# A matmul kernel's first input load issued as two transfers, of partitions 0 to 15 and 16 to 127

## The chip, the core and the metric

The kernel runs on one core of one Trainium2 chip. The metric is the device time of one execution in microseconds (us). Beside the timed runs there is one execution that the hardware profiler recorded; all rows and windows are from it, with times counted from the start of its span.

## The reference

```python
batch, m, k, n = 16, 512, 1024, 768      # all inputs float32, scale = 0.1
return (scale * np.matmul(x, weight) + add_value).astype(np.float32)
```

The 16 x 512 rows of `x` are one matrix of 8192 rows. It is multiplied by a 1024 x 768 weight, scaled, and added to an addend of 8192 x 768. Read are 33.6 MB of `x`, 3.1 MB of weights and 25.2 MB of addends; 25.2 MB are written.

## The kernel before

**Tiles.** A tile is 128 rows of `x`, one on each partition; there are 64. Partition p holds 16 rows that follow each other in memory, so a load of 8 tiles reads 8 x 4 KB = 32 KB in one run for each partition. `xs` holds 16 tiles of `x` (line 68), in four quarters of four tiles; `ao` holds 32 tiles of addends, which become results in place (line 70).

**Stages.** ScalarE (ACT) and GpSimd (POOL) are the *movers*: `mover` (lines 148 to 162) loops over turns of 16 tiles, and in a turn over the four quarters `q`. For each quarter it waits for `x_sem[q]` (line 153, the load) and `turned` (line 154, free space in `va`), and then issues eight casts that bring a quarter of `x` to bf16 in another order (line 161). VectorE (DVE) casts the weights (`cast_w`, line 167), then transposes the moved data in 32 x 32 blocks (`turn`, line 171) and later combines product and addend (`finish`, line 181). TensorE (PE) multiplies: eight weight loads and 16 matmuls for a tile (`product`, line 205; the loop at line 221). VectorE's first `turn` needs the first quarter of both movers, and TensorE needs all the weights and the first `turn`.

**Order of the transfers.** Nearly all transfers are issued by SyncE (SP), in the order of `STREAM` (line 22): `w` weights, `a` addends, `x` tiles, `o` stores, each with its first tile and count. `sync_engine` (line 95) waits ahead of a transfer for what must be free or ready, and adds 16 to a semaphore when the transfer has landed. For a load of eight tiles, `x_sem` of its first quarter counts the landing, and the semaphore of its second quarter is raised at once when it is issued (lines 145 and 146). GpSimd stores the two tiles 8 and 15 by itself, in three bands of 6, 98 and 24 partitions (`BY_POOL`, line 31).

**The first load.** Tiles 0 to 7 (`FIRST`) are not in `STREAM`. Their load is issued by SP ahead of the joined section (`tc.tile_critical`, line 240), at line 237; at line 240 SP then joins the other engines. It covers 128 partitions with 32 KB each, and raises `x_sem[0]` when it has landed. `x_sem[1]`, the semaphore of the second quarter, is raised for this load by TensorE at line 217. The last store, of tiles 60 to 63, is issued behind the section at line 252.

Of the kernel before, what the change touches and what calls it, by code (L numbers as in the profile page):

```python
# [8 lines left out]
P = 128  # L9
# [7 lines left out]
VA_BUFS = 2  # L17
MOVE = 4
AHEAD = 4
HALF_BLOCK, PAST, SYNC_AT = 64, 4, 4  # L20

STREAM = [
# [12 lines left out]
def kernel(  # L35
# [8 lines left out]
    nc = tc.nc  # L44
# [12 lines left out]
    x_v = x_f.rearrange("(g p t) k -> p g t k", p=P, t=R)  # L57
# [4 lines left out]
    def rows(view, s, n):  # L62
        assert s // R == (s + n - 1) // R
        return view[:, s // R, s % R:s % R + n, :]
# [12 lines left out]
    x_sem = [tc.alloc_semaphore(f"x{i}") for i in range(X_SLOTS // MOVE)]  # L77
# [70 lines left out]
    def mover(eng, copy, parity, count, go=None, first=0, turns=T // X_SLOTS):  # L148
        if go is None:
            eng.preload_act_table(mybir.ActivationFunctionType.Copy)  # L150
        with eng.Fori(16 * (first + 1), 16 * (first + turns) + 1, 16) as i:  # L151
            for q in range(X_SLOTS // MOVE):
                eng.wait_ge(x_sem[q], i)
                eng.wait_ge(turned, i + (4 * q - 12) if q < 3 else i)  # L154
                if go is not None:
                    eng.sem_inc(go, 1)
                k = MOVE * q
                src = xs[:, k:k + MOVE, :].rearrange("p i (c b k) -> p (i c) b k", b=4, k=64)
                for a in (parity, parity + 2):
                    for b in range(4):  # L160
                        copy(va[q % VA_BUFS][32 * b:32 * b + 32, :, a, :],  # L161
                             src[32 * a:32 * a + 32, :, b, :]).then_inc(count, 1)
# [42 lines left out]
    def product(eng, acc, x_j, w_j, j):  # L205
        eng.ldweights(x_j, tile_position=(0, 0))  # L206
        for n0, n1 in ((0, CUT), (CUT, N)):
            m = eng.add_instruction(mybir.InstMatmult(  # L208
                start_tensor_calc=(j == 0), stop_tensor_calc=(j == KJ - 1),
                tile_size=(P, P), tile_position=(0, 0), ldweights=False,  # L210
                name=nc.get_next_instruction_name(), engine=eng.engine,
                ins=[eng.lower_ap(w_j[:, n0:n1]), eng.lower_ap(x_j, for_matmul_weights=True)],
                outs=[eng.lower_ap(acc[:, n0:n1])]))
        return m

    def tensor_engine(eng):
        eng.sem_inc(x_sem[1], 16)
        eng.sem_inc(turned, TURNED)
        eng.sem_inc(made, MADE)
        eng.wait_ge(casts, KJ)  # L220
        with eng.Fori(TURNED + 2, TURNED + 2 + T, XT_TILES) as i:
            for q in range(XT_TILES):
                if q % 2 == 0:
                    eng.wait_ge(turned, i + q if q else i)
                    eng.wait_ge(made, i + q if q else i)
                for j in range(KJ):
                    x2 = xt[:, q, j // 2, :].bitcast(bf16).rearrange("p (m r) -> p r m", r=2)
                    m = product(eng, mm[:, q, :], x2[:, j % 2, :], w_bf[:, j, :], j)
                if q % 2:
                    m.then_inc(done, 4)  # L230
# [3 lines left out]
        eng.addr_align(HALF_BLOCK, offset=PAST, max_nops=0)  # L234
    s, n = FIRST
    place = dataclasses.replace(xs[:, s:s + n, :], dep_tracking_offset=P * X_SLOTS * K)
    first = nc.sync.dma_start(place, rows(x_v, s, n))
    first.then_inc(x_sem[0], 16)
    tc.no_tile_sem_insts.add(first.ins.name)
    with tc.tile_critical(no_gpsimd_drain=True):  # L240
        sync_engine(nc.sync)
        mover(nc.scalar, nc.scalar.copy, 0, by_act)
        mover(nc.gpsimd, nc.gpsimd.tensor_copy, 1, by_pool, pool_go, 0, TURN_AT)
        nc.gpsimd.wait_ge(made, MADE + PAIR.stop)
        for p, n in BY_POOL:
            store_pair(nc.gpsimd, p, n)
        nc.gpsimd.addr_align(HALF_BLOCK, offset=PAST, max_nops=0)
        mover(nc.gpsimd, nc.gpsimd.tensor_copy, 1, by_pool, pool_go, TURN_AT, T // X_SLOTS - TURN_AT)
        vector_engine(nc.vector)
        tensor_engine(nc.tensor)  # L250
    s, n = LAST
# [36 lines left out]
```

## Time and profile before

| what | value |
|---|---|
| median of 3 runs | 208.18 us (208.10 to 208.29) |
| the profiled execution's own time | 208.1 us |
| its span | 206.3 us |
| mean granted TensorE clock | 0.981 |
| bytes moved over the span | 87.04 MB, 422 GB/s |

The span is what the profiler saw between the first and the last instruction; the execution's own time holds 1.8 us more, around it. Busy shares are over the span. A row of a timeline has the start, the duration, the engine (SPq is SP's queue of issues), the line in the program, the operation, the output and the input, and in brackets the idle time before it with what ended it. A row of the chain has the start, the duration and what the time was spent on. An issue row is the time that SP takes to issue; the data move later.

### The profile page before, as it was taken

The page shows a single profiled execution, that of the slowest core. Times are in us where ns is not written, and L with a number is a line of the kernel's source. Part 1 is how long each engine was busy: PE and PEld are TensorE (multiplying, and loading weights), DVE is VectorE, ACT ScalarE, POOL GpSimd, SP SyncE. Part 2 cuts the span into 40 slices and gives each one's busy share as a digit, 9 for nine tenths or more (in the row PEclk, how much of TensorE's full clock was granted, in tenths as well). Part 3 has the DMA queues.
Part 4 walks back from the last instruction along what each step waited for, and adds up shares of the span by engine and source line. Part 5 has one row for each costly group of instructions (what it writes and reads, how often), then busy time and mean ns, then how long its engine had stood idle before and what let it go on. Part 6 is the DMA issues. An engine that isn't in the chain of part 4 may idle for free.

```text
span 206.3 us, 2222 instructions
## 1 busy us (share of the span) xinstructions
PE 168.5 (82%) x1008; PEld 50.5 (24%) x512; DVE 98.0 (48%) x66; ACT 134.7 (65%) x129; POOL 137.4 (67%) x135
## 2 busy tenths in 40 slices
PE   0000099999999999999999999999999999999800
PEld 0000023322333333223333322233333222333200
DVE  0005523555555555555555555555554655455320
ACT  2049970799999807999999069999990199910000
POOL 0049994699999906999999459999991199920000
PEclk9999999999999999999999999999999999999975
DMA  7989999999999999999999999999999999999986
GB/s 299 413 378 467 400 483 407 419 438 464 407 457 457 407 407 407 407 457 408 437 434 423 447 424 434 432 419 443 438 415 429 429 437 443 429 457 419 457 367 281
DMA packets 4065, 87.04 MB, mean 422 GB/s; under 512 B 480, under 2 KB 480, under 8 KB 1120
## 3 DMA queue, kind: packets, MB, share of 16 engines
q1 hardware_dynamic: 3856, 86.25, 97.7%
q0 software_dynamic: 208, 0.79, 0.9%
q14 instruction: 1, 0.01, 0.0%
HBM read 61.87 MB, written 25.17 MB: 422 GB/s over the span
## 4 chain that ended last, share of the span: by engine, by line
DMA 37%; PE 37%; POOL 10%; ACT 5%; issue 4%; DVE 2%; SPq 1%; POOLq 0%; DVEq 0%; ACTq 0%
PE mm L208 37%; DMA out_dram<-ao 22%; DMA xs<-in_x_dram 15%; POOL va L161 9%; ACT va L161 5%; DVE xt L176 1%; DVE ao L185 1%; POOL out_dram L93 1%; SPq L128 0%; SPq L116 0%; DVEq L174 0%; SPq L100 0%; POOLq L154 0%; POOLq L151 0%; DVEq L185 0%
## 5 line engine op out<-in xcount | busy, mean ns | idle before, releaser
L208 PE MATMUL mm<-w_bf,xt 128*128 128x256 bf16 (+1 forms) x1008 | 168.5, 328 | 27.1 <-DVE xt L176 26.2
L161 POOL CAST va<-xs 32x1024 bf16<-32x1024 f32 x128 | 135.2, 1056 | 44.3 <-DMA xs<-in_x_dram 30.6
L161 ACT CAST va<-xs 32x1024 bf16<-32x1024 f32 x128 | 133.4, 1042 | 45.3 <-DMA xs<-in_x_dram 41.7
L185 DVE SCALAR_TENSOR_TENSOR ao<-mm,ao 128x1536 f32 (+1 forms) x32 | 56.2, 1757 | 76.7 <-PE mm L208 73.6
L206 PEld LDWEIGHTS <-xt 128*128 128x128 bf16 x512 | 50.5, 99 | 144.5 <-issue 117.6
L176 DVE STREAM_TRANSPOSE xt<-va 128x1024 f32<-128x1024 f32 x32 | 39.4, 1234 | 4.6 <-POOL va L161 2.4
L169 DVE CAST w_bf<-ao 128x3072 bf16<-128x3072 f32 x2 | 4.6, 2276 | 18.0 <-DMA ao<-in_weight_dram 18.0
L150 ACT ACT_TABLE_LOAD x1 | 1.3, 1283 | 1.3 <-SPq L240 1.3
L93 POOL DMA_DIRECT2D out_dram<-ao x3 | 2.0, 672 | 0.0
L269 POOL MEMSET const-float32-0.0<- 128x1 f32 x1 | 0.1, 97 | 0.2 <-issue 0.2
L269 POOL MEMSET const-bfloat16-1.0<- 128x1 bf16 x1 | 0.1, 100 | 0.0
L269 POOL MEMSET const-float32-1.0<- 128x1 f32 x1 | 0.1, 98 | 0.0
L269 POOL MEMSET const-uint8-127<- 128x1 uint8 x1 | 0.1, 98 | 0.0
## 6 DMA issues: line engine op xcount, KB each, us to landing
xs<-in_x_dram SPq DMA_DIRECT2D x7, 4096.0 KB, 20.9
ao<-in_add_value_dram SPq DMA_DIRECT2D x6, 3072.0 KB, 16.0
out_dram<-ao SPq DMA_DIRECT2D x3, 3072.0 KB, 27.4
ao<-in_add_value_dram SPq DMA_DIRECT2D x1, 6144.0 KB, 24.2
out_dram<-ao SPq DMA_DIRECT2D x1, 6144.0 KB, 31.2
out_dram<-ao SPq DMA_DIRECT2D x1, 4608.0 KB, 14.7
xs<-in_x_dram SPq DMA_DIRECT2D x2, 2048.0 KB, 21.1
ao<-in_weight_dram SPq DMA_DIRECT2D x2, 1536.0 KB, 16.8
```

Of the source, the lines that this page charges most:

```text
L93: eng.dma_start(out_v[p:p + n, 0, PAIR, :], ao[p:p + n, PAIR, :]).then_inc(aside_sem, 16)
L150: eng.preload_act_table(mybir.ActivationFunctionType.Copy)
L161: copy(va[q % VA_BUFS][32 * b:32 * b + 32, :, a, :], src[32 * a:32 * a + 32, :, b, :]).then_inc(count, 1)
L169: eng.tensor_copy(w_bf[:, s:s + n, :], ao[:, W_AT + s:W_AT + s + n, :]).then_inc(casts, n)
L176: eng.transpose(xt[:, 2 * half:2 * half + 2, :, :].rearrange("p i c m -> p (i c m)"), va[move % VA_BUFS][:, q:q + 2 * KC, :, :].bitcast(fp ...
L185: eng.scalar_tensor_tensor(a, mm[:, q:q + 2, 0:N], float(scale), a, op0=mybir.AluOpType.mult, op1=mybir.AluOpType.add).then_inc(made, 2)
L206: eng.ldweights(x_j, tile_position=(0, 0))
L208: m = eng.add_instruction(mybir.InstMatmult(start_tensor_calc=(j == 0), stop_tensor_calc=(j == KJ - 1), tile_size=(P, P), tile_position=(0 ...
L269: nc = _bacc.Bacc("TRN2", target_bir_lowering=False, num_devices=1)
```

## The change

The load of tiles 0 to 7 is issued as two transfers, both by SP and both ahead of the joined section: partitions 0 to 15 (512 KB) with `x_sem[0]`, and partitions 16 to 127 (3584 KB) with `x_sem[1]`. The movers wait for `x_sem[0]` and `x_sem[1]` ahead of the first quarter and for no load ahead of the second. TensorE no longer raises `x_sem[1]`.

```diff
+HEAD = 16
...
         with eng.Fori(16 * (first + 1), 16 * (first + turns) + 1, 16) as i:
             for q in range(X_SLOTS // MOVE):
-                eng.wait_ge(x_sem[q], i)
+                for j in ((0, 1), (), (2,), (3,))[q]:
+                    eng.wait_ge(x_sem[j], i)
                 eng.wait_ge(turned, i + (4 * q - 12) if q < 3 else i)
...
     def tensor_engine(eng):
-        eng.sem_inc(x_sem[1], 16)
         eng.sem_inc(turned, TURNED)
...
     s, n = FIRST
     place = dataclasses.replace(xs[:, s:s + n, :], dep_tracking_offset=P * X_SLOTS * K)
-    first = nc.sync.dma_start(place, rows(x_v, s, n))
-    first.then_inc(x_sem[0], 16)
-    tc.no_tile_sem_insts.add(first.ins.name)
+    for i, part in enumerate((slice(0, HEAD), slice(HEAD, P))):
+        first = nc.sync.dma_start(place[part], rows(x_v, s, n)[part])
+        first.then_inc(x_sem[i], 16)
+        tc.no_tile_sem_insts.add(first.ins.name)
```

## Prediction, made before the result was known

> **What bounds the kernel now.** I read the page from the top: busy shares, the slices, the DMA queues. Then come windows over the start, the middle and the end, the chain, and the issues on SP in order of time.
>
> ```profile
> PE 168.5 (82%) x1008; PEld 50.5 (24%) x512; DVE 98.0 (48%) x66; ACT 134.7 (65%) x129; POOL 137.4 (67%) x135
> ...
> PEclk9999999999999999999999999999999999999975
> DMA  7989999999999999999999999999999999999986
> ...
> q1 hardware_dynamic: 3856, 86.25, 97.7%
> q0 software_dynamic: 208, 0.79, 0.9%
> ```
>
> The transfers take 98.6% of what 16 queues can carry in the span, and only the first and the last slices are below 9. No engine comes near that over the span. The windows say the same stage by stage (columns: window, its length, busy time of each engine, granted clock, DMA share, GB/s; a packet is counted where it starts, so a share can pass 1.00).
>
> ```profile
> 1.00:13.00 12.00, 0.00 (x0) 0.00 (x0) 0.00 (x0) 1.36 (x2) 0.00 (x0) 1.00 0.93 382
> 13.00:26.00 13.00, 0.00 (x0) 0.00 (x0) 5.83 (x4) 12.71 (x13) 12.39 (x10) 1.00 1.03 437
> 26.00:195.50 169.50, 168.45 (x1008) 50.54 (x512) 90.46 (x62) 120.66 (x116) 124.77 (x122) 1.00 1.00 430
> 195.50:201.00 5.50, 0.02 (x1) 0.00 (x0) 1.76 (x1) 0.00 (x0) 0.00 (x0) 0.78 0.98 424
> 201.00:203.00 2.00, 0.00 (x0) 0.00 (x0) 0.00 (x0) 0.00 (x0) 0.00 (x0) 0.50 0.99 424
> 203.00:205.00 2.00, 0.00 (x0) 0.00 (x0) 0.00 (x0) 0.00 (x0) 0.00 (x0) 0.50 0.75 320
> ```
>
> Two things run without a gap. The DMA share is 1.00 from 26 to 195.5 us and 0.98 or more up to 203. And TensorE is busy for 168.45 of the 169.50 us between its first and its last matmul, at clock 1.00. Both start behind the first load:
>
> ```profile
> 0.74 12.08 DMA xs<-in_x_dram
> ...
> 26.03 10.86 PE mm L208 x50
> ...
> 195.63 1.76 DVE ao L185
> ```
>
> These are rows of the chain: the load of tiles 0 to 7 lands at 12.82, the movers then start, TensorE starts at 26.03. The end is DMA's:
>
> ```profile
> 0.74 0.38 SPq L237 DMA_DIRECT2D xs<-in_x_dram  x1
> 1.39 0.90 SPq L109 DMA_DIRECT2D ao<-in_weight_dram  x2
> 2.34 0.58 SPq L128 DMA_DIRECT2D ao<-in_add_value_dram  x1
> 2.96 0.45 SPq L116 DMA_DIRECT2D xs<-in_x_dram  x1
> ...
> 197.67 0.33 SPq L252 DMA_DIRECT2D out_dram<-ao  x1
> ```
>
> When the last store, 1.57 MB, is issued at 197.67, the windows still have 5.33 us at 424 GB/s up to 203 and 2 us at 320 behind it, 2.26 + 0.64 = 2.9 MB. So 1.3 MB of earlier stores stand ahead of it, some 3.1 us: TensorE has that much slack at the end. **What the reader is to see:** a queue that never runs dry passes any delay at its head to the end one for one; time won at the head is passed on too. TensorE's start moves with the same load, so it does not become a new limit. The whole change lies in how soon, and how fast, the first 4 MB go in.
>
> **The change part by part.** The profiled execution took 208.1 us with a span of 206.3; the 1.8 us around it are kept. The median of the three runs is 208.18, 0.08 above. All sums are made against 208.1.
>
> 1. *Waits.* A turn of a mover had four waits on x semaphores, one for each quarter, and has four again: two at the first quarter, none at the second, one at each of the others. On SP, a full eight-tile load already raises the second quarter's semaphore at issue, so the added wait at the first quarter asks for nothing that is late in turns two to four. Behind it on ACT and GpSimd stand only the same quarter's casts. A wait on the chain costs hundredths:
>
> ```profile
> 12.84 0.04 ACTq L154
> ```
>
> In the worst case two waits in a row cost 0.04 us more for each of four turns; the queues are ahead by far more than that, so I take 0. TensorE loses one semaphore increment ahead of a wait that lasts until 26.03: 0.
>
> 2. *One more issue on SP.* The order of instructions is the same on all engines but SP, which gets a transfer of 16 x 8192 and one of 112 x 8192 for the one of 128 x 8192. The present issue takes 0.38 us, so weights, addends and tiles 8 to 15 are issued about 0.4 us later. What hides it: their data queue behind the first load, which lands only at 12.82, and SP is done issuing at 3.41. Without that cover it would be 0.4 us. The joined section is also entered 0.4 us later, and ACT's table load with it:
>
> ```profile
> 1.34 1.28 ACT L150 ACT_TABLE_LOAD   x1 [1.34 <-SPq L240]
> 12.92 17.05 ACT L161 CAST va<-xs 32x1024 bf16<-32x1024 f32 x16 [10.30 <-DMA xs<-in_x_dram]
> ```
>
> It would end at 3.0 instead of 2.62, 10 us ahead of its use: 0.
>
> 3. *The start of the queues.* Fine windows show how they start now:
>
> ```profile
> 0.00:1.70 1.70, 0.00 (x0) 0.00 (x0) 0.00 (x0) 0.36 (x1) 0.20 (x4) 1.00 0.00 0
> 1.70:1.80 0.10, 0.00 (x0) 0.00 (x0) 0.00 (x0) 0.10 (x1) 0.00 (x0) 1.00 4.58 1311
> 1.80:2.00 0.20, 0.00 (x0) 0.00 (x0) 0.00 (x0) 0.20 (x1) 0.00 (x0) 1.00 2.83 819
> 2.00:2.20 0.20, 0.00 (x0) 0.00 (x0) 0.00 (x0) 0.20 (x1) 0.00 (x0) 1.00 2.21 655
> 2.20:2.40 0.20, 0.00 (x0) 0.00 (x0) 0.00 (x0) 0.20 (x1) 0.00 (x0) 1.00 0.96 328
> 2.40:2.70 0.30, 0.00 (x0) 0.00 (x0) 0.00 (x0) 0.22 (x1) 0.00 (x0) 1.00 0.25 109
> 2.70:3.50 0.80, 0.00 (x0) 0.00 (x0) 0.00 (x0) 0.00 (x0) 0.00 (x0) 1.00 0.00 0
> ```
>
> 1311 GB/s x 0.1 us is 131 KB, four packets of 32 KB (one partition's eight tiles). The next windows hold five, four, two and one: 16 first packets, one for each queue, start between 1.7 and 2.7, with a mean of about 2.0. If 16 short lists reach all queues as soon as the first is reached now, the mean start comes 0.25 us and the last 0.8 us sooner; at the least nothing is gained. The queues rejoin at the end, so the worth lies between these: 0 to 0.8, and 0.4 if half of the spread goes.
>
> 4. *Where the first transfer goes.* This is the term that decides, and no row shows it: every load and store on SP's queue covers all 128 partitions. The first transfer uses 16 queues on 16 neighbouring partitions. The case's rows bound it from both sides. The 4.19 MB of the whole load take 9.75 us at 430 GB/s; the 0.52 MB of the first transfer take 1.22 at the same pace, the second's 3.67 MB take 8.53. **Lower end, 0:** a queue's pace is its own, wherever it writes. **Upper end:** a partition takes in no more than its 1/128 of the rate that all together show. Then 16 partitions take 53.8 GB/s and 9.75 us, 8.53 more; and the second, on 112 of 128, takes 9.75 instead of 8.53, 1.22 more; together +9.75. For the lower end speaks that the store of two tiles that GpSimd issues in bands of 6, 98 and 24 partitions shows no slower queue: 0.79 MB in 0.9% of 16 x 206.3 us is 27 GB/s for one queue, as the 86.25 MB in 97.7% give for the others. But most of it is the band of 98, it reads SBUF instead of writing it, and it runs between packets of other transfers. For the upper end speaks that the total never stays above the 430 GB/s that all 16 queues and all 128 partitions give together: nothing shows that a sixteenth of the queues could push more than a sixteenth of the total into one place, and here two queues and more would have to go into each eight partitions. Neither end has a row near it, so I take the middle, **+4.9 us**, with part 3's gain within its error (the queues' first packets would be held up anyway).
>
> [...]
>
> Sum: 208.1 + 4.9 = **213.0 us**. A queue that is held by its first packet cannot pass it, so the second transfer and the weights wait behind; the first tiles land at about 17.7 and TensorE starts at about 30.9.
>
> **The rivals.**
>
> *The queues start sooner and nothing holds them (the other side: faster).* It decides if the first transfer's 16 packets take their 1.2 us each. Then part 3 is all: 208.1 - 0.4 = 207.7, with 207.3 as its bound. For it: DMA is the bound from its first packet on, so each tenth of a microsecond counts. Against it: the gain is a part of the 1.0 us between the first and the last start, and part 4 must cost nothing. [...]
>
> *Nothing that can be measured.* The queues start as they do now, since what takes the time is the way from the issue at 0.74 to the first packet after 1.7, whatever its length; or the 16 partitions are dealt to a few queues and the other queues begin with the second transfer at once, every queue with the bytes that it has now. 208.0, with 207.8 to 208.3.
>
> *A hole between the two transfers.* The second's issue would end near 1.5 instead of 1.12, so its packets are due from about 2.1 to 3.1. The windows show no second packet before 3.5 now. The hole opens only if the second issue takes over 0.4 us more than I reckon; it would cost about 0.5: 208.6.
>
> **How the numbers follow.** Held queues (213.0): 0.58. Sooner start by over 0.2%: 0.20. Nothing measurable: 0.17. A hole: 0.05. The likeliest is the first, with its own range 210.8 to 215.0 (+2.7 to +6.9; the ends near 0 and near +9.75 are each unlikelier than the middle, and beyond 215.0 I leave 0.07). The range for 8 in 10 reaches down over the rival without effect and most of the faster one, to 207.6, and leaves 0.07 above and about 0.06 below: **207.6 to 215.0**. About 0.2%, 0.4 us, is what a measurement of this kernel can tell from no change. Faster 0.20, same 0.17, slower 0.58 + 0.05 = 0.63.
>
> **What would show it.** Right: in fine windows from 1.7 us on, 16 packets start, and then almost none up to 4 to 7 us; the chain's first piece ends near 17.7 instead of 12.82, TensorE starts near 30.9 and stays without gaps, and the last store is issued near 202.6. The windows of the middle keep share 1.00 and 430 GB/s. Wrong: the second group of 16 packets starts at 3.5 or sooner and the first load lands at 12.8 or sooner; then the first rival holds if the first 16 starts lie closer together than 1.0 us, and the second if not. If the first load lands late but the end does not move, the idea of the full queue is what failed. If the movers' first casts of a turn wait longer for a load than they do now, with the load landed, part 1 is wrong.

## The result, and the profile after

| | before | after |
|---|---|---|
| median of the timed runs | 208.11 us (208.07 to 208.29) | 217.75 us (217.53 to 218.39) |
| ratio | | 1.046, 95% interval 1.0446 to 1.0474 |
| span of the profiled execution | 206.3 us | 215.8 us |

The changed kernel is 9.6 us slower. The direction was forecast, the size was not: 213.0 was said, with 207.6 to 215.0 as the range.

The page of the changed kernel, first the rows that answer to those of before:

```profile
PE 167.3 (78%) x1008; PEld 50.3 (23%) x512; DVE 98.1 (45%) x66; ACT 134.7 (62%) x129; POOL 137.4 (64%) x135
...
DMA  7999999999999999999999999999999999999985
GB/s 115 194 285 216 402 438 474 401 422 446 462 416 428 419 425 468 401 452 433 408 416 473 431 386 437 446 427 415 433 433 431 431 434 428 492 437 405 437 387 246
...
q1 hardware_dynamic: 3872, 86.25, 97.6%
```

The busy row of the DMA queues does not show what happened: it is 9 from the second slice on, as before, and 97.6% stands where 97.7% stood. The GB/s row shows it. The first four slices, 21.6 us, move 115 to 285 GB/s; from the fifth on it is the usual 400 and more. The queues are as busy as ever, and move about half as much. Windows over the same stretches of both kernels, first before, then after (columns as in the prediction's windows):

```profile
2.70:5.00 2.30, 0.00 (x0) 0.00 (x0) 0.00 (x0) 0.00 (x0) 0.00 (x0) 1.00 0.77 328
5.00:7.00 2.00, 0.00 (x0) 0.00 (x0) 0.00 (x0) 0.00 (x0) 0.00 (x0) 1.00 0.95 410
7.00:12.00 5.00, 0.00 (x0) 0.00 (x0) 0.00 (x0) 0.00 (x0) 0.00 (x0) 1.00 0.97 419
12.00:22.00 10.00, 0.00 (x0) 0.00 (x0) 3.96 (x2) 8.88 (x9) 8.57 (x7) 1.00 1.03 433
```

```profile
2.70:5.00 2.30, 0.00 (x0) 0.00 (x0) 0.00 (x0) 0.39 (x1) 0.00 (x0) 1.00 0.00 0
5.00:7.00 2.00, 0.00 (x0) 0.00 (x0) 0.00 (x0) 0.00 (x0) 0.00 (x0) 1.00 1.47 262
7.00:12.00 5.00, 0.00 (x0) 0.00 (x0) 0.00 (x0) 0.00 (x0) 0.00 (x0) 1.00 0.82 210
12.00:22.00 10.00, 0.00 (x0) 0.00 (x0) 0.00 (x0) 0.00 (x0) 0.00 (x0) 1.00 0.94 239
22.00:36.00 14.00, 0.00 (x0) 0.00 (x0) 5.84 (x4) 12.75 (x13) 12.35 (x10) 1.00 1.02 427
36.00:205.00 169.00, 167.29 (x1008) 50.32 (x512) 90.52 (x63) 120.69 (x116) 124.82 (x122) 1.00 1.01 433
```

A packet is counted where it starts. After the 16 first packets no second one starts between 2.7 and 5.0; before, they start in this stretch at 328 GB/s. That is the small first transfer. Then come 17 us at 210 to 262 GB/s with queues that are busy nearly all the time: that is the second transfer, and it loses more than the first, as the runs below price it. From 22 us on all is as before. The chain of the changed kernel shows how it is passed on:

```profile
1.18 21.61 DMA xs<-in_x_dram
36.07 9.71 PE mm L210 x50
...
205.14 1.76 DVE ao L187
```

The first load lands at 22.79 instead of 12.82 (9.97 later), TensorE starts at 36.07 instead of 26.03 (10.04 later), its last result is 9.51 later, and the span is 9.5 longer. Half a microsecond is won back behind TensorE's start (its first 50 matmuls take 9.71 us instead of 10.86); why, no run shows. No more is won back, since neither the queues nor TensorE have a gap.

### The profile page after: what moved, and what is told of

Read it like the earlier page. It is cut to its first block, busy times and chain, and to the rows that moved or that the text cites. A ratio compares the mean times of both kernels' runs of the same rounds, so it can differ in the third digit from the quotient of the medians.

```text
span 215.8 us, 2230 instructions
## 1 busy us (share of the span) xinstructions
PE 167.3 (78%) x1008; PEld 50.3 (23%) x512; DVE 98.1 (45%) x66; ACT 134.7 (62%) x129; POOL 137.4 (64%) x135
## 3 DMA queue, kind: packets, MB, share of 16 engines
q1 hardware_dynamic: 3872, 86.25, 97.6%
## 4 chain that ended last, share of the span: by engine, by line
DMA 40%; PE 34%; POOL 9%; ACT 5%; issue 3%; DVE 3%; SPq 1%; POOLq 0%; DVEq 0%; ACTq 0%
PE mm L210 34%; DMA out_dram<-ao 21%; DMA xs<-in_x_dram 19%; POOL va L163 9%; ACT va L163 5%; DVE xt L178 2%; DVE ao L187 1%; POOL out_dram L94 1%; SPq L129 0%; SPq L239 0%; SPq L117 0%; DVEq L176 0%; SPq L101 0%; POOLq L156 0%; POOLq L158 0%
## 6 DMA issues: line engine op xcount, KB each, us to landing
xs<-in_x_dram SPq DMA_DIRECT2D x1, 3584.0 KB, 21.6
```

## The experiments

Theory 1 was the prediction's: where in SBUF the 16 queues write at a time decides their pace. Against it stood that any second transfer or wait at the head costs, that any transfer of fewer than 128 partitions is slow, that the small first transfer alone is slow, and that the memory which is read decides. The ratios below are to the kernel before, run beside each.

### The waits alone

One load of 128 partitions, with the changed waits of the movers.

```diff
-    for i, part in enumerate((slice(0, HEAD), slice(HEAD, P))):
...
+    first = nc.sync.dma_start(place, rows(x_v, s, n))
+    first.then_inc(x_sem[0], 16)
...
+        eng.sem_inc(x_sem[1], 16)
```

> The changed kernel's waits of the movers alone (both semaphores at the first quarter, none at the second); one load of 128 partitions, and TensorE raises the second semaphore as before. All theories of the transfers: 208.1, within 0.1. If the waits cost anything: up to 0.3 more.

Measured: 208.13 us, ratio 0.9996 (0.9987 to 1.0005). The waits cost nothing; all of the loss is in the transfers.

### The same cut in bytes, by tiles

```diff
-HEAD = 16
+HEAD = 1
...
-    for i, part in enumerate((slice(0, HEAD), slice(HEAD, P))):
-        first = nc.sync.dma_start(place[part], rows(x_v, s, n)[part])
+    for i, part in enumerate((slice(0, HEAD), slice(HEAD, n))):
+        first = nc.sync.dma_start(place[:, part, :], rows(x_v, s, n)[:, part, :])
```

> The changed kernel, with the same two transfers of 512 KB and 3584 KB, the same issues, semaphores and waits, but cut by tiles: tile 0 on all 128 partitions, then tiles 1 to 7 on all 128. Theory 1 (the place in SBUF): nothing is lost, 207.8 to 208.5. Rival (a second transfer at the head, or the second wait, costs by itself): near 217.5.

Measured: 208.79 us, ratio 1.0029 (1.0017 to 1.0041), a little above what was expected. Two transfers of the same sizes cost 0.6 us, not 9.6, as long as each covers all partitions.

### The cut at 64, and the cut into even and odd partitions

```diff
-HEAD = 16
+HEAD = 64
```

> The changed kernel with the cut at partition 64 instead of 16. Theory 1: partitions 0 to 63 hold half of the ways in, so each half goes at half the pace and the first load lands near 22 us: 217 to 218. If what costs is the small first transfer of 16 partitions, the loss is less than with 16: 210 to 213.

Measured: 218.54 us, ratio 1.0497 (1.0481 to 1.0513), a little above what was expected; the first load lands at 23.58 us. The other cut into 64 and 64:

```diff
-    for i, part in enumerate((slice(0, HEAD), slice(HEAD, P))):
+    for i, part in enumerate((slice(0, P, 2), slice(1, P, 2))):
```

> The changed kernel with the load cut into the even and the odd partitions, 64 each: as many transfers, partitions and bytes as with the cut at 64, but each half lies on all of SBUF. Theory 1 (neighbouring partitions share a way in): the loss goes, 208.5 to 209, as with the cut by tiles. Rival (a transfer of fewer than 128 partitions is slow by itself): 218 to 219 as with the cut at 64.

Measured: 208.51 us, ratio 1.0022 (1.0011 to 1.0032). These two kernels have the same number of transfers, partitions, pieces and bytes, and the same waits. They differ in which partitions go together (and with them which rows of `x`), and that is worth 10 us. A small first transfer is not needed for the loss: with 64 and 64 it is even larger.

### The shapes one at a time

Twelve loads ahead of the kernel's first load, each waited for; the one below stands for all:

```diff
+        nc.sync.dma_start(xs[0:16, s:s + n, :], rows(x_v, s, n)[0:16]).then_inc(probe_sem, 16)
+        nc.sync.wait_ge(probe_sem, 32)
```

> The kernel before, with twelve loads of tiles 0 to 7 issued one at a time ahead of its own first load (each waited for; all are written over by the full load at the end), so that the time of each shape stands alone. Order: partitions 0-127; 0-15; 16-127; every 8th partition (16 of them); 0-15 from every 8th row block; every 8th partition from row blocks 0-15; 0-31; 0-63; every 2nd partition (64); 0-95; 0-111; 32-95. Theory 1, neighbouring partitions share a way into SBUF that carries about one queue's pace, so the place decides: 11 us for the 128; about 6 for 0-15 wherever its rows come from; clearly less, 3 to 4, for every 8th partition wherever its rows come from; 15 to 18 for 16-127; about 6 for 0-31 and 11 for 0-63; less than 11 for every 2nd partition. Theory 2, a transfer that is not 128 partitions is slow by itself: about 6 for every 8th partition as for 0-15, and the same for all the 64s. Theory 3, the memory that is read decides: 0-15 from every 8th row block is as fast as every 8th partition, and every 8th partition from row blocks 0-15 as slow as 0-15.

The kernel was executed once, in 328.81 us. In its chain each load is a row (start, duration), in the order above; the rows of 0.02 us of issue between them are left out here:

```profile
0.95 12.02 DMA xs<-in_x_dram
12.99 6.71 DMA xs<-in_x_dram
19.72 16.86 DMA xs<-in_x_dram
36.60 4.96 DMA xs<-in_x_dram
41.58 6.62 DMA xs<-in_x_dram
48.21 4.71 DMA xs<-in_x_dram
52.94 7.03 DMA xs<-in_x_dram
59.98 12.54 DMA xs<-in_x_dram
72.55 7.58 DMA xs<-in_x_dram
80.15 16.41 DMA xs<-in_x_dram
96.57 16.65 DMA xs<-in_x_dram
113.24 7.56 DMA xs<-in_x_dram
```

The first three rows are partitions 0 to 127, 0 to 15 and 16 to 127: a load of 112 partitions takes 4.84 us longer than one of all 128. The next three rows are 16 partitions each: every eighth, 0 to 15 filled from every eighth row block, and every eighth filled from row blocks 0 to 15. Where the rows come from hardly matters (6.71 and 6.62; 4.96 and 4.71); where they go does, though every eighth was expected to take 3 to 4 us and took 4.96. Partitions 0 to 63 and 32 to 95 are 64 each: the same size, 12.54 and 7.56. For a rate I take off 2.27 us, what a full load needs beyond its 9.75 us at 430 GB/s:

| partitions loaded | MB | issue to landing, us | GB/s without the 2.27 us |
|---|---|---|---|
| 0-127 | 4.19 | 12.02 | 430 |
| 0-15 | 0.52 | 6.71 | 118 |
| every 8th (16) | 0.52 | 4.96 | 195 |
| 0-31 | 1.05 | 7.03 | 220 |
| 0-63 | 2.10 | 12.54 | 204 |
| even ones (64) | 2.10 | 7.58 | 395 |
| 32-95 | 2.10 | 7.56 | 396 |
| 0-95 | 3.15 | 16.41 | 222 |
| 0-111 | 3.67 | 16.65 | 255 |
| 16-127 | 3.67 | 16.86 | 252 |

The rivals fall: the number of partitions does not decide (64 of them run at 204, 395 or 396 GB/s), and neither does the source for 16 partitions, the only size for which it was varied. 0 to 63 is no faster than 0 to 31 (204 and 220). And 0 to 111, which holds all of 32 to 95 and 48 partitions more, runs at 255 where 32 to 95 run at 396: that a shape is fast does not make a larger one around it fast. The way into SBUF that theory 1 speaks of, and what one carries, was the author's guess: these runs time whole shapes.

That the slow shapes simply use fewer queues is not the reason either, as the packets of the two kernels show. The 16 that start between 1.70 and 2.70, first before, then after:

```profile
1.70:2.70 1.00, 0.00 (x0) 0.00 (x0) 0.00 (x0) 0.92 (x1) 0.00 (x0) 1.00 1.73 524
```

```profile
1.70:2.70 1.00, 0.00 (x0) 0.00 (x0) 0.00 (x0) 0.89 (x1) 0.00 (x0) 1.00 3.64 524
```

A share of 3.64 of 16 queues over 1.00 us is 3.64 us of a queue for each of 16 packets; before it is 1.73. For the second transfer, 210 GB/s between 7 and 12 us are 32 packets of 32 KB in 0.82 of 16 x 5.00 us, 2.05 us of a queue for each; before, 419 GB/s are 64 packets in 0.97 of it, 1.21 for each. The queues are busy (97.3% from 5.0 to 22.8 us after), and each packet takes longer.

### The two transfers of the change, priced apart in the kernel

The kernel before, with one more transfer ahead of its first load:

```diff
+    extra = nc.sync.dma_start(
+        dataclasses.replace(xs[0:16, 8:16, :], dep_tracking_offset=2 * P * X_SLOTS * K), rows(x_v, 8, 8)[0:16])
+    extra.then_inc(extra_sem, 16)
...
+                need(extra_sem, 16)
                 move = eng.dma_start(xs[:, k:k + n, :], rows(x_v, s, n))
```

> The kernel before, with its first load in one piece, and one more transfer ahead of it: partitions 0 to 15 of tiles 8 to 15, which the next load of x writes again later (its issue waits for this one). It prices the small transfer of the change alone. Theory 1: its 0.52 MB hold the queues for 4.4 us, as it took 6.71 by itself where 2.3 of the 12.02 of a full load are not data: 212.4 to 213. Rival (a small transfer costs its bytes, and the loss is in the second one): 209.4.

Measured: 212.45 us, ratio 1.0201 (1.0184 to 1.0218), 4.28 above the 208.17 beside it. The bytes cost 1.22 at the full pace; 3.1 are lost. With `16:P` in place of `0:16`:

> The same with partitions 16 to 127 of tiles 8 to 15, which prices the second transfer of the change alone. Theory 1 with what the single loads showed: 16.86 less 2.3, +14.5, 222 to 223, which is 6 more than its bytes cost. Rival (only the first, small transfer is slow, and what follows it waits): its bytes at the full pace, +8.5, 216.7.

Measured: 222.19 us, ratio 1.0672 (1.0654 to 1.069), 14.02 more. The bytes cost 8.53; 5.5 are lost. So the small transfer loses 3.1 and the large one 5.5, together 8.6 of the 9.6. The single loads gave 3.2 and 6.1. About 1 us is missing. Part of it is what each run wins back behind the landing of the first load: by the landings, 17.48 and 27.19 against 12.82, the two lose 3.4 and 5.8, 9.3 of the 9.97. No run takes the rest apart.

### More shapes, stores, and sizes of pieces

> The kernel before with fourteen single transfers ahead of its first load, each waited for. Loads: partitions 0-127; 0-15; 64-79; 56-71; every 4th (32); 16-79; 64-127; the odd ones (64); 16-111; 8-127. Then stores of 3 KB pieces of what was loaded (the output is written again later): 0-127; 0-15; 16-127; the even ones. [...] If a store's reading of SBUF is held in the same way, 0-15 and 16-127 of the stores are slower than their bytes say, as with the loads (9.6, 4 to 5, 12 to 13, 6); if only writing is held, about 9.6, 3.2, 9, 6.

Measured, loads from issue to landing: 12.01, 6.90, 6.93, 6.67, 5.01, 12.60, 12.73, 7.48, 16.45 and 22.11 us. The loads of 64 to 79 and of 56 to 71 are as slow as 0 to 15 (6.93 and 6.67 beside 6.90), and every fourth, 32 partitions, takes 5.01 where 0 to 31 took 7.03. 16 to 79 and 64 to 127 (12.60 and 12.73) are like 0 to 63 of the first dozen (12.54), the odd ones (7.48) like the even ones (7.58), and 16 to 111 (16.45) like 0 to 95 (16.41). One stands out: 8 to 127, 120 partitions, takes 22.11, nearly twice as long as all 128; why, no run shows. That load and the four stores, of 0 to 127, 0 to 15, 16 to 127 and the even ones, in the chain (rows of issue left out):

```profile
87.89 22.11 DMA xs<-in_x_dram
110.03 9.31 DMA out_dram<-xs
119.36 5.16 DMA out_dram<-xs
124.53 9.97 DMA out_dram<-xs
134.52 5.83 DMA out_dram<-xs
```

Stores are held as well: an eighth of the bytes takes 5.16 us from partitions 0 to 15, half of them from the even ones 5.83. For stores no run varied where the rows go in memory. But 16 to 127 lose far less than as a load. To tell whether it was the size of the pieces or the direction:

> The kernel before with nine single transfers ahead of its first load, each waited for: a load of partitions 0-127 in pieces of 32 KB; loads in pieces of 3 KB of 0-127, 0-15, 16-127 (three quarters of the bytes); stores in pieces of 24 KB of 0-127, 0-15, 16-127, the even ones; the load of 16-127 in pieces of 32 KB again. It is to tell why stores of 16-127 lost less (9.97 beside 9.31) than loads (16.86 beside 12.02): piece size or direction. If long pieces let the queues collide: the loads of 3 KB pieces lose little with 16-127 (about 10 beside 9.6) and the stores of 24 KB much (13 to 14 beside 9.3). If writing SBUF is what collides: the 3 KB loads lose much (13 beside 9.6), the 24 KB stores little (10). 0-15 is held to about a quarter of the pace in all cases (4.5 to 5.5).

```profile
13.04 10.38 DMA xs<-in_x_dram
23.44 5.59 DMA xs<-in_x_dram
29.05 12.88 DMA xs<-in_x_dram
41.95 8.71 DMA out_dram<-xs
50.67 5.11 DMA out_dram<-xs
55.80 9.82 DMA out_dram<-xs
65.64 5.37 DMA out_dram<-xs
71.02 17.23 DMA xs<-in_x_dram
```

These are the loads of 0 to 127, 0 to 15 and 16 to 127 in pieces of 3 KB, then the stores of the same and of the even ones in pieces of 24 KB, then the load of 16 to 127 in pieces of 32 KB again (rows of issue left out). Short pieces do not save the load of 112 (12.88 beside 10.38), and long ones do not hurt the store more (9.82 beside 8.71). The direction decides: a load of 112 partitions loses much, a store of the same little. That it is the writing of SBUF, and not the reading of memory, fits the loads of 16 partitions, where the source hardly mattered, but was not shown for 112. The repeated load took 17.23 us beside 16.86, so a single load is known to some 0.4 us. The kernels of these two sections were executed once each, in 348.17 and 295.79 us.

### What the end hangs on

Tiles 0 to 3 and 4 to 7 as two transfers of all partitions, each quarter's casts waiting for its own:

```diff
-    for i, part in enumerate((slice(0, HEAD), slice(HEAD, P))):
-        first = nc.sync.dma_start(place[part], rows(x_v, s, n)[part])
+    for i, part in enumerate((slice(0, MOVE), slice(MOVE, n))):
+        first = nc.sync.dma_start(place[:, part, :], rows(x_v, s, n)[:, part, :])
...
-                for j in ((0, 1), (), (2,), (3,))[q]:
-                    eng.wait_ge(x_sem[j], i)
+                eng.wait_ge(x_sem[q], i)
```

> The kernel before with its first load cut into tiles 0 to 3 and tiles 4 to 7, each on all 128 partitions, and each quarter's casts waiting for their own part alone. It tells whether the end hangs on the queues or on TensorE's start. The first casts should start near 8 us instead of 12.9 and TensorE 0.5 to 2 us sooner (the weights hold it then). If the queues set the end, as the prediction read it: 208.2 to 208.8, the price of a cut and no gain. If TensorE's start sets it: 206.5 to 207.7.

Measured: 208.05 us, ratio 0.9993 (0.9984 to 1.0002). Its timeline:

```profile
8.06 17.04 ACT L161 CAST va<-xs 32x1024 bf16<-32x1024 f32 x16 [4.96 <-DMA xs<-in_x_dram]
...
23.45 6.79 PE L208 MATMUL mm<-w_bf,xt 128*128 128x512 bf16 x27 [23.45 <-DVE xt L176]
```

The casts start 4.9 us sooner and TensorE 2.6 us sooner (0.5 to 2 were expected), and the time does not move; nor is the last store issued sooner (198.04 instead of 197.67). An earlier start of TensorE is lost again: between 26 and 195 us it is busy for 166.01 of 169.00 us, with a DMA share of 1.01, where before it was busy for 168.45 of the 169.50 from 26 to 195.5. That it waits for transfers there, so that the queues set the pace, is a reading; no row here names the waits. No run delays TensorE alone, so the slack that the prediction read for it at the end is not tested. This cut cost nothing that can be measured, not even the price that was expected, unlike that of tile 0 alone (0.6 us) and the even and odd one (0.3). In the even and odd one the first load lands at 13.14 us instead of 12.82, about as much later as it loses: its first half takes SP 0.55 us to issue instead of 0.38, and 15 packets start between 1.7 and 2.7 us (492 GB/s) where before 16 did (524). Why tile 0 alone loses, no run shows. No run points to a version that beats the kernel before.

## Why the prediction was right or wrong

- *What bounds the kernel: right.* The queues never run dry, a delay at their head arrives at the end but for half a microsecond (9.97 late at the landing, 9.5 at the end), and an earlier start of TensorE alone is worth nothing (2.6 us sooner, ratio 0.9993). No run won time at the head of the queues, so that such a gain is passed on too was not shown. The 3.1 us of slack come from a mean rate that holds 2 us from before the last store's issue; from 197.67 on the trace has 8.63 us at 319 GB/s, 2.75 MB, which leaves 1.2 MB or 2.8 us. No run tests it.
- *Part 1, waits at 0: right*, by the kernel with the waits alone.
- *Part 2, the second issue hidden: right.* SP takes 0.85 us for the two, the weights are issued at 1.86 instead of 1.39, and this is behind a full queue:

```profile
0.74 0.85 SPq L239 DMA_DIRECT2D xs<-in_x_dram  x2
1.81 1.28 ACT L151 ACT_TABLE_LOAD   x1 [1.81 <-SPq L242]
1.86 1.07 SPq L110 DMA_DIRECT2D ao<-in_weight_dram  x2
```

- *Part 3, a sooner start worth 0 to 0.8: 0.* The first 16 packets of the changed kernel start in the same stretch:

```profile
1.70:1.80 0.10, 0.00 (x0) 0.00 (x0) 0.00 (x0) 0.00 (x0) 0.00 (x0) 1.00 11.55 1638
1.80:2.00 0.20, 0.00 (x0) 0.00 (x0) 0.00 (x0) 0.19 (x1) 0.00 (x0) 1.00 3.52 492
2.00:2.20 0.20, 0.00 (x0) 0.00 (x0) 0.00 (x0) 0.20 (x1) 0.00 (x0) 1.00 2.24 328
2.20:2.40 0.20, 0.00 (x0) 0.00 (x0) 0.00 (x0) 0.20 (x1) 0.00 (x0) 1.00 3.33 492
2.40:2.70 0.30, 0.00 (x0) 0.00 (x0) 0.00 (x0) 0.30 (x1) 0.00 (x0) 1.00 2.22 328
```

  1638 GB/s x 0.1 us and so on are 5, 3, 2, 3 and 3 packets, between 1.7 and 2.7 as before. A shorter list did not bring the queues closer together, so even without the loss the change had nothing to win.
- *Part 4, the step that failed.* That the place in SBUF holds the queues was right (218.54 us with the cut at 64, 208.51 with the even and the odd ones), and the sign that was named came: 16 first packets, then none up to 5.0 us. What failed is the term for the second transfer. It was given 0 to 1.22 us, as if a transfer could at most be slowed by its share of the partitions, 7/8 here; it loses 5.5 to 6.1, more than half of the 9.6, so 1.22 was no upper end. The first was given 0 to 8.53; it loses 3.1 to 3.2. The middle put 4.3 on the first and 0.6 on the second. That the upper end of the sum, +9.75, lies beside the measured 9.6 is chance: a share of 1/128 for each partition would give the load of 0 to 31 another 9.75 us of data, and it took 4.8. The middle of two far ends was a choice without a row; and the range, cut at 215.0, left out an upper end of 217.9 that the working itself had set.
- *The rivals.* A sooner start, nothing measurable, and a hole all assumed queues at their own pace, and fell with that.
- *What stays open:* why transfers of 96, 112 and 120 partitions go at about half the pace. 0 to 95 run at 222 GB/s, 0 to 111 at 255, and 8 to 127 take 22.11 us, beside 430 GB/s and 12.02 us for all 128; 32 to 95, which lie inside all three, run at 396. The trace does not name the partition of a packet, so the cause stays open.

## What to carry to other kernels

Cut a load by tiles and leave each part all 128 partitions (here 0.6 us more at most, beside 9.6 and 10.3 for the cuts at partitions 16 and 64), or test the shape by itself: a dozen single loads in one run, each waited for, price every shape to some 0.4 us. When the queues bound a kernel, read GB/s beside the busy share, since a queue that is held is busy too (share 0.94 at 239 GB/s here). And where the working has an upper end that no row excludes, the range has to reach it.

## What the runs showed of the hardware that was not expected

A load of 120 partitions took 22.11 us and one of 112 took 16.86, beside 12.02 for all 128: leaving partitions out made the transfer longer. Stores from 16 neighbouring partitions are slow too (an eighth of the bytes from 0 to 15 took 5.16 us, all of them 9.31), but a store of 112 partitions lost little where a load lost much (9.82 beside 8.71 us, 16.86 beside 12.02). And a queue that is held counts as busy: share 0.94 at 239 GB/s.
